# Eleven tiny SyncE loads and sixteen small GpSimd loads added in mid-kernel to a rotary-embedding score kernel

## The chip, the cores and the metric

The kernel runs on one core of one Trainium2 chip. The time is device microseconds of one launch. What lies in a profile is one execution; the timed runs are others of the same program.

## The reference

Queries and keys of 16 batches, 512 positions, 16 heads and 64 elements are rotated by position-dependent cosines and sines, and for every batch and position the 16 heads' queries are multiplied with the keys of the same head:

```python
q_rot = concat([q1 * cos - q2 * sin, q1 * sin + q2 * cos])   # q1, q2: halves of the 64 elements
k_rot = concat([k1 * cos - k2 * sin, k1 * sin + k2 * cos])
scores = einsum('bshd,bthd->bsht', q_rot, k_rot)             # fp32, 16 x 512 x 16 x 512
```

The output has 268 MB, the two inputs 67 MB together; both go through the core's DMA engines once.

## The kernel before

The 512 positions of a batch are dealt over 128 partitions, four to a partition: `C = 4`. A step handles one such quarter of a batch, 128 query positions against all 512 key positions for all 16 heads, so there are `NST = 64` steps, four a batch. The first four (batch 0) have a form of their own with smaller loads and stores; the others, from step 4 to step 63, are one loop.

In a step `i` of the loop, `scores(i, p, st)` runs for eight pairs of heads `p`: two matrix products into a PSUM tile (line 166), and a ScalarE copy of both into the staging tile `st` (line 173). Between the pairs, TensorE transposes the rotated queries of step `i + 1` and a quarter of the keys of the batch after (line 127), and VectorE or ScalarE copies them out of PSUM (line 142). VectorE's rotations (lines 106, 107 and 111) for the steps ahead are woven in between, the rest of them in `run(dve)` at the end of the step.

After the last pair of a step, `store(i, st)` writes the staging tile, 4 MB, to `out`. A staging tile is 32 KB a partition, and there are three of them (`stage_pool`, `bufs=3`), so ScalarE's first copy of step `i` waits until the store of step `i - 3` has landed. Two steps, `NST - 8 = 56` and `NST - 1 = 63`, write in three pieces: all 128 rows of most heads, then 116 rows and 12 rows of the last two (step 56) or three (step 63) heads:

```python
nc.sync.dma_start(o[:, :h], st[:, :h])
nc.sync.dma_start(o[:116, h:], st[:116, h:])
nc.sync.dma_start(o[116:, h:], st[116:, h:])
```

At the end of step `i`, after `run(dve)`, the loop issues a load: with `i % 4 == 2` the queries of batch `i // 4 + 2`, with `i % 4 == 3` the keys of batch `i // 4 + 3`, each 2 MB, into one of two buffers. Step 50 thus issues the queries of batch 14, step 54 those of batch 15. All loads and stores but two at the start (`cos`, `sin`) are issued by SyncE, in program order: store 50, the queries of batch 14, store 51, a load of keys, stores 52, 53 and 54, the queries of batch 15, store 55, the three pieces of step 56, and so on. Nothing is issued by GpSimd, which only builds the identity matrix at the start.

The order of the instructions on each engine is that of the program text (`tc.manual_schedule()`); the waits between engines and DMAs are put in by the framework from what each instruction reads and writes.

Of the kernel before, what the change touches and what calls it, by code (L numbers as in the profile page):

```python
# [10 lines left out]
def kernel(  # L11
# [8 lines left out]
    nc = tc.nc  # L20
    fp32 = mybir.dt.float32
# [5 lines left out]
    P = 128  # L27
    C = S // P
    HP = H // 2
    NST = B * C  # L30
    G = H // C

    const_pool = ctx.enter_context(tc.tile_pool(name="const", bufs=1))
# [16 lines left out]
    cos_t = const_pool.tile([P, C, HD], fp32, name="cos_t")  # L50
# [2 lines left out]
    ss_v = ss_t.rearrange("p c x j -> p c (x j)")  # L53

    st_first = [stage_pool.tile([P, H, S], fp32, tag="stage", name="st") for _ in range(2)]
    early = stage_pool.tile([P, 2 * C * H * D], fp32, tag="stage", name="early")
# [3 lines left out]
    def load_units(which, head, heads):  # L62
        n = C * heads * D
        t = early[:, used[0] : used[0] + n].rearrange("p (c e) -> p c e", c=C)
        used[0] += n
        src = dram[which][0, :, :, head : head + heads, :]
        nc.sync.dma_start(t.rearrange("p c (h d) -> p c h d", d=D), src)
        for h in range(0, heads, G):
            units[which, (head + h) // G] = t[:, :, D * h : D * (h + G)]
# [3 lines left out]
    def load(which, b):  # L73

        if b >= B:
            return
        t = in_pool.tile([P, C, H * D], fp32, tag=which + "_in", name=which + "_sb")
        batches[which, b] = t
        nc.sync.dma_start(t.rearrange("p c (h d) -> p c h d", h=H), dram[which][b])

    def rope(which, n):

        part = part_pool.tile([P, H * D], fp32, tag="part", name="part")
        if n < C:
            x = units[which, n]
            sv, k1, k2 = "p c (g j) -> p c g j", {"j": HD}, {"j": D}
            cs = cos_t.unsqueeze(2).to_broadcast((P, C, 2 * G, HD))
            ss = ss_v.unsqueeze(2).to_broadcast((P, C, G, D))
            pv = part.rearrange("p (c g j) -> p c g j", c=C, j=D)  # L90
            x5 = x.rearrange("p c (h x j) -> p c h x j", x=2, j=HD)
            p5 = part.rearrange("p (c h x j) -> p c h x j", c=C, x=2, j=HD)
            adds = [(x5[:, :, :, y], p5[:, :, :, 1 - y]) for y in range(2)]
        else:
            x = batches[which, n // C][:, n % C]
            sv, k1, k2 = "p (g j) -> p g j", {"j": HD}, {"j": D}
            cs = cos_t[:, n % C].unsqueeze(1).to_broadcast((P, 2 * H, HD))
            ss = ss_v[:, n % C].unsqueeze(1).to_broadcast((P, H, D))
            pv = part.rearrange(sv, **k2)
            x4 = x.rearrange("p (h x j) -> p h x j", x=2, j=HD)  # L100
            swapped = bass.AP(part.tensor, part.offset + HD, [part.ap[0], (D, H), (-HD, 2), (1, HD)])
            adds = [(x4, swapped)]
        xs, xc = x.rearrange(sv, **k2), x.rearrange(sv, **k1)

        def products():
            nc.vector.tensor_tensor(pv, xs, ss, op=mult)  # L106
            nc.vector.tensor_tensor(xc, xc, cs, op=mult)  # L107

        def sums():
            for y, z in adds:  # L110
                nc.vector.tensor_tensor(y, y, z, op=add)  # L111

        return [products, sums]
# [41 lines left out]
    def scores(i, p, st):  # L155

        ps = ps_s_pool.tile([P, 2, S], fp32, tag="ps_s", name="ps")
        b = i // C
        if b == 0:
            c, hp = divmod(p, 2)  # L160
            lhs, rhs = qT[i][:, C * hp + c], kT[0][:, 2 * i + hp]
        else:
            lhs, rhs = qT[i][:, p], kT[b][:, p]
        for r in range(2):
            po, rh = ps[:, r, :], rhs[64 * r : 64 * r + 64, :]
            nc.tensor.matmul(  # L166
                out=po, lhsT=lhs[64 * r : 64 * r + 64, :], rhs=rh, start=True, stop=True
            )
        so, si = st[:, 2 * p : 2 * p + 2, :], ps
        if b > 0:  # L170
            so = so.rearrange("s r (t c) -> s r t c", c=C)
            si = si.rearrange("s r (c t) -> s r t c", c=C)
        nc.scalar.copy(out=so, in_=si)  # L173
        if b == 0 and p % 2 == 1:
            c = p // 2
            nc.sync.dma_start(o_v[0, c, :, G * i : G * (i + 1)], st[:, G * c : G * (c + 1)])
        elif b > 0 and p == HP - 1:
            store(i, st)

    def tr_act(which, n):  # L180
        for g in range(2):
            transposed(which, n, g, nc.scalar.copy)

    def run(ops):
        for op in ops:
            op()

    with tc.manual_schedule():
        for t, src in ((cos_t, cos), (sin_t, sin)):
            nc.scalar.dma_start(t, src.rearrange("(p c) j -> p c j", c=C))  # L190
        for head, heads in ((0, G), (G, H - G)):
            load_units("k", head, heads)
            load_units("q", head, heads)
        load("k", 1)
        load("q", 1)
        make_identity(nc, ident)
        nc.scalar.copy(out=ss_t[:, :, 0, :], in_=sin_t)
        nc.scalar.mul(ss_t[:, :, 1, :], sin_t, -1.0)  # L198
        for which in ("k", "q"):
            run(rope(which, 0))  # L200
            tr_act(which, 0)

        for i in range(C):
            st = st_first[i] if i < 2 else stage_pool.tile([P, H, S], fp32, tag="stage", name="st")
            if i < C - 1:
                dve = rope("k", i + 1) + rope("q", i + 1) + rope("k", C + i)
                nxt = [("k", i + 1), ("q", i + 1)]
            else:
                dve = rope("q", C) + rope("k", C + i) + rope("q", C + 1) + rope("k", 2 * C)  # L210
                nxt = [("q", C), ("k", C + i)]
            for p in range(HP):
                scores(i, p, st)
                if p in (0, 1) and i > 0:
                    run(dve[:1])
                    dve = dve[1:]
                    transposed("k", C + i - 1, p, nc.vector.tensor_copy)
                if p == 3 and i < 2:
                    load("kq"[i], 2)
                if p in (2, 6):  # L220
                    m = len(dve) - (4 if p == 2 else 2) - (2 if i == C - 1 else 0)
                    run(dve[:m])
                    dve = dve[m:]
                    tr_act(*nxt.pop(0))
            run(dve)
        load("k", 3)

        for i in range(C, NST):
            tr = {}  # L230
            if i + 1 < NST:
                tr[1], tr[3] = ("q", i + 1, 0), ("q", i + 1, 1)
            if i + C < NST:
                tr[5], tr[6] = ("k", i + C, 0), ("k", i + C, 1)
            dve = []
            if i + 2 < NST:
                dve += rope("q", i + 2)
            if i + 1 + C < NST:
                dve += rope("k", i + 1 + C)
            st = stage_pool.tile([P, H, S], fp32, tag="stage", name="st")  # L240
            for p in range(HP):
                scores(i, p, st)
                if p not in tr:
                    continue
                if tr[p][0] == "q":
                    run(dve[:1])
                    dve = dve[1:]
                    transposed(*tr[p], nc.vector.tensor_copy)
                else:
                    transposed(*tr[p], nc.scalar.copy)  # L250
            run(dve)
            if i % C == C - 2:
                load("q", i // C + 2)
            elif i % C == C - 1:
                load("k", i // C + 3)
# [30 lines left out]
```

## Time and profile before

| | us |
|---|---|
| median of 2 runs (799.76 and 801.14) | 800.45 |
| profiled execution, span from its first to its last instruction | 798.6 |
| TensorE busy | 690.1 (86%) |
| ScalarE busy | 561.3 (70%) |
| VectorE busy | 544.5 (68%) |
| GpSimd busy | 0.7 |
| mean DMA rate | 421 GB/s |
| a 4 MB store, issue to landing, median | 24.1 |
| a 2 MB load, issue to landing, median | 27.6 |

The profiled execution has no time of its own beside its span; the two runs lie 1.2 and 2.5 us above the span, for what comes before the first and after the last instruction. Busy times of different engines overlap. TensorE's busy time counts pipelined matrix products whose ends are modelled. A DMA's time from issue to landing includes its time in the queue behind the DMAs issued before it.

### The profile page before, as it was taken

The page shows a single profiled execution, that of the slowest core. Times are in us where ns is not written, and L with a number is a line of the kernel's source. Part 1 is how long each engine was busy: PE and PEld are TensorE (multiplying, and loading weights), DVE is VectorE, ACT ScalarE, POOL GpSimd, SP SyncE. Part 2 cuts the span into 40 slices and gives each one's busy share as a digit, 9 for nine tenths or more (in the row PEclk, how much of TensorE's full clock was granted, in tenths as well). Part 3 has the DMA queues.
Part 4 walks back from the last instruction along what each step waited for, and adds up shares of the span by engine and source line. Part 5 has one row for each costly group of instructions (what it writes and reads, how often), then busy time and mean ns, then how long its engine had stood idle before and what let it go on. Part 6 is the DMA issues. An engine that isn't in the chain of part 4 may idle for free.

```text
span 798.6 us, 7719 instructions
## 1 busy us (share of the span) xinstructions
PE 690.1 (86%) x3072; PEld 299.2 (37%) x3072; DVE 544.5 (68%) x516; ACT 561.3 (70%) x647; POOL 0.7 (0%) x6
## 2 busy tenths in 40 slices
PE   4999998997979789797897988979889798899970
PEld 2444443433434334343343433424334243344420
DVE  7999987676857568575685766857758577586300
ACT  3888886776848668485785866858668586688770
POOL 0000000000000000000000000000000000000000
PEclk9999999899989899898998998999989899899995
DMA  9999999999999999999999999999999999999995
GB/s 357 421 411 435 437 423 433 423 427 440 421 431 429 429 437 427 436 421 434 426 432 434 431 420 429 434 429 437 427 424 407 443 422 440 423 404 419 426 426 235
DMA packets 17988, 336.17 MB, mean 421 GB/s; under 512 B 1824, under 2 KB 3104, under 8 KB 4384
## 3 DMA queue, kind: packets, MB, share of 16 engines
q1 hardware_dynamic: 17664, 335.55, 98.7%
q8 instruction: 24, 0.39, 0.2%
q10 hardware_dynamic: 288, 0.13, 0.1%
q14 instruction: 12, 0.10, 0.0%
HBM read 67.24 MB, written 268.44 MB: 420 GB/s over the span
## 4 chain that ended last, share of the span: by engine, by line
DMA 51%; PE 38%; ACT 4%; DVE 3%; issue 1%; ACTq 0%; SPq 0%
DMA out_dram<-st 48%; PE ps L166 29%; PE bank L127 9%; ACT st L173 4%; DMA q_sb<-in_q_dram 2%; DVE part L106 1%; DMA sin_t<-in_sin_dram 0%; DVE q_sb L107 0%; DVE k_sb L111 0%; DVE k_sb L107 0%; DVE q_sb L111 0%; DVE early L107 0%; DVE kT_t L142 0%; ACTq L281 0%; DVE early L111 0%
## 5 line engine op out<-in xcount | busy, mean ns | idle before, releaser
L173 ACT COPY st<-ps 128x1024 f32<-128x1024 f32 x512 | 495.0, 1019 | 203.4 <-DMA out_dram<-st 112.3
L166 PE MATMUL ps<-kT_t,qT_t 64*128 64x512 f32 x2048 | 547.9, 653 | 72.1 <-ACT st L173 72.1
L166 PEld LDWEIGHTS ps<-kT_t,qT_t 64*128 64x128 f32 x2048 | 185.0, 197 | 261.9 <-issue 140.6
L142 DVE COPY qT_t<-bank 128x512 f32<-128x512 f32 x118 | 81.5, 691 | 203.8 <-PE bank L127 203.8
L127 PEld LDWEIGHTS bank<-ident,q_sb 128*128 128x128 f32 x480 | 55.5, 151 | 102.4 <-issue 99.8
L127 PE MATMUL bank<-ident,q_sb 128*128 128x128 f32 x480 | 86.7, 308 | 0.9 <-PE ps L166 0.9
L127 PEld LDWEIGHTS bank<-ident,k_sb 128*128 128x128 f32 x480 | 50.5, 141 | 95.0 <-DVE k_sb L107 37.5
L127 PE MATMUL bank<-ident,k_sb 128*128 128x128 f32 x480 | 78.7, 287 | 1.2 <-DVE qT_t L142 1.2
L142 ACT COPY kT_t<-bank 128x512 f32<-128x512 f32 x122 | 72.5, 599 | 6.2 <-PE bank L127 6.2
L107 DVE TENSOR_TENSOR q_sb<-q_sb,cos_t 128x1024 f32<-128x1024 f32 x60 | 73.5, 1225 | 2.1
L111 DVE TENSOR_TENSOR k_sb<-k_sb,part 128x1024 f32<-128x1024 f32 x60 | 73.5, 1225 | 2.1
L107 DVE TENSOR_TENSOR k_sb<-k_sb,cos_t 128x1024 f32<-128x1024 f32 x60 | 73.5, 1225 | 2.0
L106 DVE TENSOR_TENSOR part<-q_sb,ss_t 128x1024 f32<-128x1024 f32 x60 | 73.5, 1225 | 2.0
L106 DVE TENSOR_TENSOR part<-k_sb,ss_t 128x1024 f32<-128x1024 f32 x60 | 73.0, 1216 | 0.1
L111 DVE TENSOR_TENSOR q_sb<-q_sb,part 128x1024 f32<-128x1024 f32 x60 | 72.9, 1216 | 0.0
L127 PE MATMUL bank<-ident,early 128*128 128x128 f32 x64 | 10.5, 316 | 12.3 <-DVE early L111 10.4
L127 PEld LDWEIGHTS bank<-ident,early 128*128 128x128 f32 x64 | 8.3, 161 | 17.3 <-issue 13.2
L106 DVE TENSOR_TENSOR part<-early,ss_t 128x1024 f32<-128x1024 f32 x8 | 9.8, 1223 | 5.7 <-ACT ss_t L198 5.5
L111 DVE TENSOR_TENSOR early<-early,part 128x512 f32<-128x512 f32 x16 | 10.3, 687 | 0.2
L107 DVE TENSOR_TENSOR early<-early,cos_t 128x1024 f32<-128x1024 f32 x8 | 9.8, 1225 | 0.3
L142 ACT COPY qT_t<-bank 128x512 f32<-128x512 f32 x10 | 5.7, 630 | 3.2 <-PE bank L127 3.2
L142 DVE COPY kT_t<-bank 128x512 f32<-128x512 f32 x6 | 4.1, 684 | 0.0
(9 smaller groups left out, 2.8 us busy)
## 6 DMA issues: line engine op xcount, KB each, us to landing
out_dram<-st SPq DMA_DIRECT2D x58, 4096.0 KB, 24.1
k_sb<-in_k_dram SPq DMA_DIRECT2D x15, 2048.0 KB, 27.6
q_sb<-in_q_dram SPq DMA_DIRECT2D x15, 2048.0 KB, 27.6
out_dram<-st SPq DMA_DIRECT2D x16, 1024.0 KB, 13.7
out_dram<-st SPq DMA_DIRECT2D x1, 3584.0 KB, 22.8
out_dram<-st SPq DMA_DIRECT2D x1, 3328.0 KB
early<-in_k_dram SPq DMA_DIRECT2D x1, 1536.0 KB, 8.8
early<-in_q_dram SPq DMA_DIRECT2D x1, 1536.0 KB, 12.0
```

What stands on the lines that cost most here:

```text
L106: nc.vector.tensor_tensor(pv, xs, ss, op=mult)
L107: nc.vector.tensor_tensor(xc, xc, cs, op=mult)
L111: nc.vector.tensor_tensor(y, y, z, op=add)
L127: nc.tensor.transpose(bank[:, x, :], src, ident)
L142: copy(out=dst, in_=src)
L166: nc.tensor.matmul(out=po, lhsT=lhs[64 * r : 64 * r + 64, :], rhs=rh, start=True, stop=True)
L173: nc.scalar.copy(out=so, in_=si)
```

## The change

Two small helpers are added, and called in three places. `probe(counts)` issues tiny loads on SyncE, each of 8 columns (32 bytes) of a few rows of `cos` into a tile of its own; the count 1 stands for 17 rows. `burden()` makes one small ScalarE copy into a tile `sw`, and then sixteen times [...]issues a GpSimd load of 17 rows, two pieces of 104 elements (416 bytes) each, into the same part of `sw`. Nothing reads `hw` or `sw` afterwards. Step 50 gets the loads of 5 to 11 rows and the sixteen GpSimd loads, between `run(dve)` and the load of the queries of batch 14; step 54 gets the loads of 17, 2, 3 and 4 rows, ahead of the load of the queries of batch 15. All else stays.

```diff
+    hw = [const_pool.tile([P, 8], fp32, name=f"hw{n}") for n in range(12)]
+    sw = const_pool.tile([P, 224], fp32, name="sw")
+    PROBE = NST - 14
+
+    def probe(counts):
+        for n in counts:
+            rows = 17 if n == 1 else n
+            nc.sync.dma_start(hw[n][:rows, :], cos[:rows, :8])
+
+    def burden():
+        nc.scalar.copy(out=sw[:, :8], in_=cos_t[:, 0, :8])
+        for n in range(16):
+            nc.gpsimd.inc_swdge_sem([], [], mode="reset_dge_cursor")
+            src = bass.AP(q.tensor, 2048 * n, [(4096, 17), (512, 2), (1, 104)])
+            nc.gpsimd.dma_start(sw.rearrange("p (a b) -> p a b", a=2)[:17, :, :104], src)
...
             run(dve)
+            if i == PROBE:
+                probe((5, 6, 7, 8, 9, 10, 11))
+                burden()
+            if i == PROBE + 4:
+                probe((1, 2, 3, 4))
             if i % C == C - 2:
                 load("q", i // C + 2)
```

## The prediction

> **What bounds the kernel now.** I read the page first, then SyncE's own waits, its timeline around step 50, the store's line, and the stages.
>
> ```profile
> span 798.6 us, 7719 instructions
> ...
> DMA  9999999999999999999999999999999999999995
> ...
> q1 hardware_dynamic: 17664, 335.55, 98.7%
> ...
> DMA 51%; PE 38%; ACT 4%; DVE 3%; issue 1%; ACTq 0%; SPq 0%
> ...
> L173 ACT COPY st<-ps 128x1024 f32<-128x1024 f32 x512 | 495.0, 1019 | 203.4 <-DMA out_dram<-st 112.3
> ```
>
> The reader is to see a kernel held by the 16 DMA engines: they are busy in every slice, nearly all of it with SyncE's queue (q1), and ScalarE's largest idle time ends when a store lands and frees a staging buffer. So whatever makes a DMA engine idle or gives it more work is paid, unless that engine has slack.
>
> The page hides that the 16 engines are not level. The trace's landing events show each engine's share of a store: store 49 lands between 635.00 and 645.53 us, store 50 between 644.75 and 655.54. Ten to eleven shares come within about a microsecond of the first; one engine trails by 10.8 us. Leading engines keep their lead only while the queue holds work. The laggard is not the one that ends the kernel: it has its last full share at 790.32, while the four engines that carry the 116-row pieces of steps 56 and 63 run to 797.28. They are busy without a gap from 708 us on.
>
> ```profile
> SPq L147 <- ACT st L173: 645.8, 58, 16.3
> ```
>
> ```profile
> L147 SPq EVENT_SEMAPHORE  x58: 17/17/17, 62.9 to 757.4; - x58
> L147 SPq DMA_DIRECT2D out_dram<-st x58: 332/332/360, 73.2 to 766.9; - x58
> ...
> DMA to landing us min/median/max: 16.5/24.1/30.3
> ```
>
> The first line is the longest of SyncE's own waits (total, times, longest): the stores wait for ScalarE, and no wait for a DMA is listed but the final one. The others are the store's line. Each of the 58 whole stores has one event-semaphore instruction ahead of it. In the trace's operands it waits for the semaphore that the store itself will raise when it lands. SyncE's DMAs take eight such semaphores in turn (I call them lanes 0 to 7), so a DMA is issued only once the DMA eight places earlier has landed. With eight DMAs reaching back some 50 us against a largest landing time of 30.3, this costs nothing today, and no such wait is in the list.
>
> ```profile
> 630.07 0.33 SPq L147 DMA_DIRECT2D out_dram<-st  x1
> 630.50 0.66 SPq L79 DMA_DIRECT2D q_sb<-in_q_dram  x1
> 647.02 0.33 SPq L147 DMA_DIRECT2D out_dram<-st  x1
> 647.45 0.45 SPq L79 DMA_DIRECT2D k_sb<-in_k_dram  x1
> 657.04 24.43 SPq L147 DMA_DIRECT2D out_dram<-st  x3
> 681.57 0.82 SPq L79 DMA_DIRECT2D q_sb<-in_q_dram  x1
> ```
>
> Those are store 50, the q load of batch 14, store 51, a k load, stores 52 to 54, the q load of batch 15. The seven step-50 loads of the change go between the first two lines.
>
> ```profile
> 635.76 2.84 ACT L173 COPY st<-ps 128x1024 f32<-128x1024 f32 x3 [5.72 <-DMA out_dram<-st]
> ```
>
> ```profile
> 646.00:658.00 12.00, 12.00 (x60) 5.23 (x56) 9.40 (x9) 10.67 (x13) 0.00 (x0) 1.00 1.01 436
> 658.00:700.00 42.00, 36.87 (x155) 15.49 (x153) 27.02 (x26) 27.41 (x32) 0.00 (x0) 0.88 1.00 430
> ```
>
> First ScalarE's timeline at the end of step 50, then two stages; DMA share and GB/s stand last. There is no DMA hole at 646 to 658 today.
>
> [...] one 4-byte completion packet per engine used makes 112 x 16 for all full DMAs, ACT's two among them, plus 4 + 12 + 4 + 12 for the split ones, 1824, the page's count under 512 B. The 12-row piece's shares land 0.18 us after the 116-row piece's on the same four engines. No run here shows a GpSimd DMA. [...]
>
> **Part 1: the SyncE loads and their lanes.** Store 50 holds lane 7. The 5 to 11-row loads take lanes 0 to 6, whose earlier holders are store 45, store 46, a q load, store 47, a k load, store 48 and store 49. The first five have landed by 625.7. The sixth load waits for store 48 (635.66), the seventh for store 49 (645.53). Behind them stands the q load, which now falls on lane 7 itself and waits for store 50, the DMA issued just before: 655.54 instead of 630.50. Store 51, its data ready at 647.02, stands behind that. So the ring holds nothing after store 50 but rows of 32 B.
>
> The leading engines finish store 50 at 644.75 and start again at 657.5 (issue at 655.6, then the 2.0 us that store 47 took from its issue at 598.38 to its first share's start, 610.10 less eight packets of 1.213). That is 12.7 us of idle. The laggard idles 2 us. Afterwards all are level. Can the four final engines win it back? In the kernel before they had about 0.45 us of further starvation (at 698 to 708), so no. Their ends lay between 795.6 and 797.3 because of their own lag of up to 1.7 us, which the pause levels: all arrive at about 797.3 + 12.7 - 0.45 - 1.7 = 807.9. That is +10.6. I checked the rest of the chain for a second hole: store 51 now lands at about 673 (before 670.4), store 54 is issued near 683, the next ones at some 699, 707 and 719, each 8 us or more before the ring runs dry.
>
> The issues themselves, 7 x 0.33 to 0.66 us and 4 more at step 54, lie in SyncE's own idle time (631 to 647, and after 682, with work queued until about 696). At step 54 the lanes asked for hold store 51 and the k load, landed by about 680: nothing. The descriptors are 27 on the first engine, at 9 ns (4-byte packets) to 27 ns (512-byte ones): 0.2 to 0.7, I take 0.3 us. If the pause weren't there, these issues would still cost nothing.
>
> **Part 2: ScalarE's copy** of 128x8 is below the 0.6 us of a 128x512 one, and falls into its 5.72 us of waiting at 630 to 636: nothing.
>
> **Part 3: the GpSimd loads.** 16 loads of 17 rows x 2 pieces of 416 B are 544 packets. Packet times are 27 ns at 512 B, 46 at 1 KB, 309 at 8 KB, 1213 at 32 KB, or some 8 ns + 37 ns per KB: 23 to 24 ns each, 0.83 us a load, 13.2 us in all. [...] all of them weigh on one engine, which I take to be the first: one of the four that end the kernel. All write the same tile, so I expect each to wait for the one before. One load then takes: descriptor making and landing, bounded by the 1.6 us from issue to first landing of the small cos load[...], 0.8 us of packets, and one to four turns behind a 1.2 us store packet. That is 3 us in the pause and 4.5 to 8 us otherwise. From 631 to 657.5 I count 4.5 loads; those are hidden by the pause. The other 11.5 x 0.83 = 9.5 us are added to an engine that never idles again. The chain ends near 735, well before the kernel. Bounds: 0 (all inside the pause, or another engine) to 13.2; above if packets are dearer.
>
> **Sum.** 10.6 + 0.3 + 9.5 = 20.4 us on a span of 798.6, or 819.0. The median of the runs, 800.45, lies 1.85 above the span; the same surplus gives 820.9, so 821.
>
> **Rivals.** *A, mostly the pause (chance 0.32).* The GpSimd loads are dealt two rows to an engine (nine engines, 64 packets each: 1.5 us), or are not serialized and run in the pause. [...] Time 800.45 + 10.9 + 1.5 = 812.9. This is the case on the other side, within 2%: it decides once fewer than six loads (5.1 us / 0.83) run after 657.5.
>
> *B, the chain outlives the kernel (0.15).* If an engine alternates single pieces with 32 KB store packets, a load takes 34 x 1.24 = 42 us plus 3. By 808 about seven are done; the other nine take 3.5 us each in an empty queue, 32 us: 842. For: store packets are single rows. [...]
>
> *C, SyncE isn't held (0.06),* because small shapes raise their lanes otherwise. Then only GpSimd's 13.2 us or 1.5 remain: 801 to 814. Against: the wait instruction is on every store.
>
> **Chances.** Main case 0.45, and 0.02 for something that helps. Of the main case 0.05 stays below 816.5 (some 2%, about what a measurement here can tell from no change). Slower: 0.40 + 0.15 + 0.03 of unnamed mishaps = 0.58; same: 0.05 + 0.32 + 0.03 = 0.40; faster 0.02. The range reaches from 808, below A with a cheap restart, to 842, B's value.
>
> **What would show it.** SyncE's waits list DMA waits of about 13 and 10 us at the small loads and the q load; the q load's issue at about 655.6; DMA share far below 1 between 646 and 658; packets below 512 B up by 544 + 16 x 16 and the small rows; the last store's landing near 817; later in the kernel ScalarE waiting for stores that one engine holds back. Wrong, if the q load is still issued near 634, if the GpSimd packets end before 660, or if they run on after the last store.

## The result, and the profile after

The changed kernel took 821.81 us (821.03 and 822.59) against 800.45 before: 1.027 of it, with an interval of 1.0236 to 1.0304, or 21.4 us more. The prediction said 821. The total is met more closely than its terms: the pause was put some 3 us too low and the GpSimd loads some 3 us too high, as the experiments show.

The page of the changed kernel, the lines that answer to those of before and two more:

```profile
span 819.3 us, 7767 instructions
...
DMA  9999999999999999999999999999999499999993
GB/s 358 420 424 430 433 419 439 420 432 429 431 435 429 425 430 434 431 425 438 421 434 428 429 436 427 436 423 432 434 424 434 204 392 435 394 422 375 424 406 133
...
q1 hardware_dynamic: 17812, 335.55, 96.6%
q0 software_dynamic: 1280, 0.26, 0.2%
```

The DMA row was full from end to end; now its 32nd slice of forty (635 to 655 us) is at 4, with 204 GB/s. After it the rate stays below that of before although the busy digit is 9 again. Those are two places to look for the loss: a hole, and slower going after it. The new queue q0, GpSimd's, has 1280 packets, which is 16 loads x 16 engines x 5. By their sizes in the trace a load has three packets of 4160 B and one of 1664 B, which are ten, ten, ten and four pieces of 416 B; 45 packets of 40 B and 15 of 16 B, which fits three and one for each of the fifteen other engines; and 16 completion packets of 4 B. SyncE's queue q1 has 148 packets more than before, 82 rows of 32 B and 66 completion packets of 4 B, both of 9 ns (median). By the landing events each tiny load has a share for every row, but that of 17 rows a single one (landed 710.54): 56 + 9 + 1 = 66.

SyncE's own waits in the changed kernel (total, times, longest), and its timeline:

```profile
SPq L64 <- DMA out_dram<-st: 10.0, 2, 9.4
SPq L95 <- DMA out_dram<-st: 9.9, 1, 9.9
```

```profile
628.49 0.33 SPq L163 DMA_DIRECT2D out_dram<-st  x1
628.88 15.53 SPq L64 DMA_DIRECT2D hw<-in_cos_dram  x7
654.37 0.36 SPq L95 DMA_DIRECT2D q_sb<-in_q_dram  x1
654.83 0.38 SPq L163 DMA_DIRECT2D out_dram<-st  x1
655.31 0.37 SPq L95 DMA_DIRECT2D k_sb<-in_k_dram  x1
655.77 29.89 SPq L163 DMA_DIRECT2D out_dram<-st  x3
```

Line 64 is the tiny load, line 95 the load of queries or keys, line 163 the store. The seven tiny loads stretch over 15.5 us, because the last two wait: the sixth for store 48 (landed 634.10, load issued 634.12), the seventh for store 49 (landed 644.10, issued 644.12). The load of queries behind them is issued at 654.37, 0.07 us after store 50's last share landed (654.30 by the landing events); in the kernel before it stood 0.43 us behind the store's own issue. By the operands in the trace the seven tiny loads wait for the semaphores 100, 101, 102, 103, 105, 107 and 109, each for the one that it raises itself, and ahead of the load of queries stands a wait for 110, which is store 50's. Store 51 and the keys follow at once: they had been ready, and were held only by SyncE's order.

The stages of the changed kernel (busy time of each engine, then granted clock, DMA share, GB/s):

```profile
632.00:646.00 14.00, 10.73 (x44) 4.69 (x44) 6.73 (x6) 9.85 (x12) 0.96 (x1) 0.88 0.85 359
646.00:658.00 12.00, 12.00 (x58) 5.18 (x57) 10.37 (x10) 10.15 (x12) 1.93 (x2) 1.00 0.30 93
658.00:700.00 42.00, 31.35 (x132) 13.49 (x132) 23.04 (x22) 23.56 (x28) 3.64 (x4) 0.84 1.01 423
700.00:730.00 30.00, 24.80 (x114) 10.38 (x111) 19.70 (x19) 20.64 (x25) 2.14 (x3) 0.91 1.00 408
```

In 646 to 658 TensorE is busy for all of the 12 us and ScalarE for 10, while the DMA share is 0.30, against 1.01 in the same stage of the kernel before: nothing that computes was late, only the DMA queue was empty. There is a second, smaller hole: from 751 to 754 the DMA share is 0.35 at 144 GB/s, after ScalarE had waited 6.44 and 3.77 us for stores (until 726.65 and 741.19) and a store was issued only at 753.24. The slowest engines had work all the while: the store before lands on the first engine at 751.0 and on the last at 761.0. GpSimd's timeline, in part (in brackets the idle time before a load and what ended it):

```profile
640.75 0.96 POOL L71 DMA_DIRECT2D sw<-in_q_dram  x1 [10.82 <-DMA sw<-in_q_dram]
651.99 0.96 POOL L71 DMA_DIRECT2D sw<-in_q_dram  x1 [10.27 <-DMA sw<-in_q_dram]
656.08 0.96 POOL L71 DMA_DIRECT2D sw<-in_q_dram  x1 [3.12 <-DMA sw<-in_q_dram]
666.10 0.96 POOL L71 DMA_DIRECT2D sw<-in_q_dram  x1 [9.06 <-DMA sw<-in_q_dram]
...
798.29 0.96 POOL L71 DMA_DIRECT2D sw<-in_q_dram  x1 [11.80 <-DMA sw<-in_q_dram]
```

Each load waits for the one before. The third, issued at 651.99 while most engines are idle, lands 3.8 us later; behind stores a load takes about 11 us (median of the sixteen 11.5). In the sixth load, behind stores, the four large packets start at 681.38, 682.74, 684.11 and 685.48, each as long after the one before as one of them and one 32 KB store packet take (0.16 + 1.21 us); in the third they start at 653.69, 653.85, 654.13 and 654.29, one after another. Thirteen come after the hole, and the last lands at 809.8, before the last store piece at 818.3.

### The profile page after: what moved, and what is told of

Read it like the earlier page. It is cut to its first block, busy times and chain, and to the rows that moved or that the text cites. A ratio compares the mean times of both kernels' runs of the same rounds, so it can differ in the third digit from the quotient of the medians.

```text
span 819.3 us, 7767 instructions
## 1 busy us (share of the span) xinstructions
PE 690.4 (84%) x3072; PEld 300.2 (37%) x3072; DVE 544.6 (66%) x516; ACT 561.7 (69%) x648; POOL 16.2 (2%) x22
## 3 DMA queue, kind: packets, MB, share of 16 engines
q0 software_dynamic: 1280, 0.26, 0.2%
## 4 chain that ended last, share of the span: by engine, by line
issue 95%; POOL 2%; POOLq 0%
POOL sw L71 2%; POOLq L302 0%; POOLq L69 0%; POOL ident masks.py:199 0%; POOL ident masks.py:197 0%; POOLq masks.py:199 0%; POOLq L291 0%
## 5 line engine op out<-in xcount | busy, mean ns | idle before, releaser
L122 DVE TENSOR_TENSOR part<-k_sb,ss_t 128x1024 f32<-128x1024 f32 x60 | 73.0, 1216 | 0.1
L127 DVE TENSOR_TENSOR q_sb<-q_sb,part 128x1024 f32<-128x1024 f32 x60 | 72.9, 1216 | 0.0
L71 POOL DMA_DIRECT2D sw<-in_q_dram x16 | 15.5, 970 | 782.4 <-ACT sw L67 627.6
```

Of the source, the lines that this page charges most:

```text
L71: nc.gpsimd.dma_start(sw.rearrange("p (a b) -> p a b", a=2)[:17, :, :104], src)
```

## The experiments

Theory: eight landing semaphores taken in turn (lanes; in the trace of the changed kernel 100 to 103, 105, 107, 109 and 110, with 15 or 16 DMAs each) make SyncE wait, the wait empties the DMA engines, and the GpSimd loads then weigh on one engine that ends the kernel. Rivals: the pause is won back, the pause is all, the loads cost by their mere count. Ratios are to runs of the kernel before on the same chip.

**The SyncE loads alone.** The line `burden()` is left out.

> The eleven tiny SyncE loads at steps 50 and 54 alone, without the ScalarE copy and the GpSimd loads. Theory (lane pause): the queries' load still waits for store 50, the 16 engines run dry between about 643 and 657 us, and the kernel takes 800.45 + 10.9 = about 811 us; in the profile the load is issued in the same tenth of a microsecond in which store 50 lands. Rival (the GpSimd loads make nearly all of the 21 us, the pause is won back by later slack): within 3 us of 800. Rival (the pause makes nearly all): 818 or more.

Measured 815.0 us, 1.0170 (1.0153 to 1.0187): 14.1 more than the 800.9 beside it. The load of queries is issued at 656.17, store 50's last share had landed at 656.09, and two stages of it read

```profile
646.00:660.00 14.00, 14.00 (x68) 5.92 (x64) 11.67 (x12) 12.15 (x14) 0.00 (x0) 1.00 0.29 97
660.00:700.00 40.00, 29.62 (x125) 12.61 (x125) 21.62 (x22) 22.18 (x27) 0.00 (x0) 0.83 1.01 424
```

The profiled execution is the longest of the four (818.25 us, with a span of 816.5). The pause is there without any GpSimd load, and it isn't won back. It costs 3 us more than expected, about its whole length: the first share of store 50 lands at 644.95, the first share of the load of queries at 663.90. Its eight packets take 0.611 us each in a full queue, so 14.0 us lie between 644.95 and the 659.0 at which they would have had to start.

**The GpSimd loads alone.** Both calls of `probe` are left out.

> The ScalarE copy and the 16 GpSimd loads at step 50 alone, no tiny SyncE loads. Theory (one engine that ends the kernel takes all the data): no pause, so all 16 loads are paid, at 0.55 us of packets each (in the profile of the changed kernel: three of 161 ns and one of 69 ns)[...]: 16 x 0.85 = 13.6, about 814 us. If the engine were one with slack of 7 to 9 us at the end: 805 to 808. Rival (the pause is all): 800 to 802. If both parts simply add, this and the run with the SyncE loads alone give together the 21.4 us of the whole change; with three loads hidden in the pause their sum should be 2 to 3 us more.

Measured 812.99, 1.0147 (1.0120 to 1.0174). The number is near the expected one, the reason only half so. Of the 0.85 us a load behind it 0.55 is measured (three packets of 161 ns and one of 69); the other 0.3, here and at step 30, was the author's estimate, shown by no trace. And in the profiled execution, the longest of the four at 815.19, the last store piece landed at 808.2, and the chain of loads ended at 811.9, after it. GpSimd's last two loads:

```profile
801.47 0.96 POOL L71 DMA_DIRECT2D sw<-in_q_dram  x1 [9.92 <-DMA sw<-in_q_dram]
809.17 0.97 POOL L71 DMA_DIRECT2D sw<-in_q_dram  x1 [6.74 <-DMA sw<-in_q_dram]
```

So 3.7 us of that execution are a chain that outlives the stores, as in rival B of the prediction; in the changed kernel the stores end later and hide it. How much of the median's 12.1 us it makes wasn't measured. The two parts alone make 14.1 + 12.1 = 26.2 us, 4.8 more than the whole change, where 2 to 3 more were expected.

**Five tiny loads.** At step 50 `probe((5, 6, 7, 8, 9))`, nothing else of the change.

> Only five of the tiny loads at step 50 (5 to 9 rows), nothing at step 54 and no GpSimd loads. Lane theory: the queries' load then stands on the lane of store 48 (landed at about 635), store 51 on that of store 49 (landed at 645, before its data are ready at 647), the keys' load on that of store 50, which still leaves it 2 us before the queue runs dry. So no pause: 800 to 801 us, although five of the seven loads are there. Rival (tiny loads themselves disturb the engines, each by about 1.5 us): 808.

**Six tiny loads.** At step 50 `probe((5, 6, 7, 8, 9, 10))`, nothing else.

> As the run with five, with the load of 10 rows added: six. Lane theory: the queries' load waits for store 49 (about 645.5), 2.8 us of empty queue on the leading engines, and store 51 waits for store 50 (about 655.5), 5.1 us more after the queries have been loaded: 7.9 us of pause less 2 us of lag that it levels, about 806 us. Rival (each tiny load costs the same): a seventh of the way more than with five, about 809 to 810, in line with it. Rival (only the wait of the queries' load counts): 802.

Five: 801.10, 1.0004 (0.9996 to 1.0013), no difference. Six: 808.34, 1.0091 (1.0076 to 1.0107), 2 us more than expected. SyncE's timeline of the two around step 50, five first:

```profile
631.30 0.33 SPq L163 DMA_DIRECT2D out_dram<-st  x1
631.69 4.83 SPq L64 DMA_DIRECT2D hw<-in_cos_dram  x5
636.63 1.15 SPq L95 DMA_DIRECT2D q_sb<-in_q_dram  x1
645.36 0.37 SPq L163 DMA_DIRECT2D out_dram<-st  x1
654.63 0.33 SPq L95 DMA_DIRECT2D k_sb<-in_k_dram  x1
```

```profile
629.55 0.33 SPq L163 DMA_DIRECT2D out_dram<-st  x1
629.93 5.88 SPq L64 DMA_DIRECT2D hw<-in_cos_dram  x6
645.48 0.36 SPq L95 DMA_DIRECT2D q_sb<-in_q_dram  x1
655.53 0.37 SPq L163 DMA_DIRECT2D out_dram<-st  x1
656.00 0.37 SPq L95 DMA_DIRECT2D k_sb<-in_k_dram  x1
```

With five, the keys' load waits for store 50 (landed 654.6), and still comes in time; with six, the load of queries waits for store 49 and store 51 for store 50. The stage 646 to 658, five and then six:

```profile
646.00:658.00 12.00, 12.00 (x60) 5.46 (x60) 9.91 (x10) 10.15 (x13) 0.00 (x0) 1.00 1.03 437
```

```profile
646.00:658.00 12.00, 12.00 (x60) 5.30 (x58) 9.40 (x10) 10.67 (x13) 0.00 (x0) 1.00 0.70 274
```

Nothing, 7.4 and 14.1 us for five, six and seven at step 50: a threshold and then a step for each load, where a cost by the load would have shown at five. Each load more moved every DMA behind it one place closer to the one that it had to wait for: the load of queries is issued at 636.63 with five, at 645.48 behind store 49 with six, and at 656.17 behind store 50 with seven.

**The same eleven, dealt.** `probe((5, 6, 7, 8, 9))` at step 50, `probe((1, 2, 3, 4))` at step 54, `probe((10, 11))` at step 58, no `burden()`.

> All eleven tiny SyncE loads, but those of 10 and 11 rows moved from step 50 to the end of step 58; no ScalarE copy and no GpSimd loads. Lane theory: with five at step 50, four at step 54 and two at step 58 every lane that is asked for has landed, or just lands, so no pause: 800 to 802 us, against 815 for the same eleven loads with seven of them at step 50. Rival (the loads' descriptors and issues cost it): about 815 again.

Measured 800.87, 1.0007 (1.0000 to 1.0015). All eleven loads together cost 0.6 us by the ratio and 1.2 at most by its interval, where no more than five stand in a row. The lane theory passes its sharpest test here: the same loads cost 14.1 us when seven stand in a row.

**Step 56 stored whole** (an edit of the kernel before).

```diff
-        if i not in (NST - 8, NST - 1):
+        if i != NST - 1:
```

> The kernel before with one edit: step 56 is stored whole, as the other steps are, instead of in three pieces; no tiny and no GpSimd loads. It tells which engines end the kernel before. As the prediction read the landings (only the four engines with the 116-row pieces end it, the laggard is done at 790.32): those four lose 5.9 + 0.2 us of pieces and get 1.2 us of whole rows, so about 796. As I read them now, with the extra semaphore events put aside (the laggard[...] has its last full share at 797.0, as late as the four): the laggard gets 8 x (1.213 - 1.062) us more and saves its one 12-row packet of 0.2, so 801 to 802, or 0.1% slower.

Measured 800.16, 1.0000 (0.9992 to 1.0009). The first reading, 796, falls. The second's direction can't be told at this size, but the landings agree with it: the laggard's last full share lands at 797.1, the four engines end between 795.7 and 796.8.

**Pieces of one element.** In `burden()`, `(1, 104)` becomes `(1, 1)` and `[:17, :, :104]` becomes `[:17, :, :1]`.

> The changed kernel with each GpSimd piece cut from 104 elements (416 B) to one (4 B); 16 loads of 34 pieces as before, so the load's count, its waits and its turns stay, its bytes go. The changed kernel took 21.4 us more than before, the SyncE loads alone 14.1 in the run with them alone: the GpSimd loads' own part is about 7. Theory (the bytes on one engine): the 13 loads after the pause lose 13 x 0.5 us of packets, so about 815. Rival (turns: a load breaks into the stores' queue on every engine, whatever its size): unchanged, 821. In between, some 817 to 818, if both count.

**No cursor reset.** The line `nc.gpsimd.inc_swdge_sem(...)` is left out.

> The changed kernel without the 16 resets of the GpSimd cursor; the loads are the same. Theory (with the reset all data go to one engine, without it they go round): each engine gets the data of one load, 0.55 us, instead of one engine that of 16; about 816. Rival (the cursor has no part in where the data go, or the engine has no part in the cost): unchanged, 821.

Without bytes: 820.21, 1.0246 (1.0231 to 1.0261). Without resets: 821.18, 1.0270 (1.0245 to 1.0295). Both intervals overlap that of the changed kernel. So neither the bytes nor their lying on one engine make most of the GpSimd part; the theory in this form falls. The run without bytes also has fewer packets, two a load on every engine (136 B and 4 B) instead of five, and its chain of loads ends at 770.3 instead of 809.8; still it costs 5.2 us more than the SyncE loads alone. So the number of packets doesn't make most of it either. What stays is 34 pieces a load on every engine, if one reads the sizes so, which is the author's reading: 136 B is 34 x 4, and 40 and 16 B on the other engines are 10 x 4 and 4 x 4. No run here varied the number of pieces. The stages of the run without bytes, at the same distance from the pause as those of the SyncE loads alone, show what is left:

```profile
660.00:700.00 40.00, 28.86 (x116) 12.33 (x116) 21.20 (x20) 20.57 (x24) 4.82 (x5) 0.79 1.01 419
700.00:740.00 40.00, 36.67 (x170) 15.79 (x166) 28.25 (x27) 29.35 (x35) 3.86 (x4) 0.96 1.00 404
```

against this second stage of the SyncE loads alone:

```profile
700.00:740.00 40.00, 35.83 (x164) 15.33 (x160) 29.67 (x28) 27.76 (x34) 0.00 (x0) 0.96 1.00 426
```

The engines are busy all the time in both, and move 426 or 404 GB/s. Between 700 and 780 us the stores' 32 KB packets take 1219 ns in the mean in the run with the SyncE loads alone and 1251 in the one without bytes, the loads' 16 KB packets 621 and 726.

**A place of its own for each load.** In `burden()`, `[:17, ...]` becomes `[r : r + 17, ...]` with `r = 17 * (n % 7)`.

> The changed kernel with the GpSimd loads written to seven groups of 17 partitions in turn instead of all to the first 17, so that up to seven are in flight and none waits for the one just before it. [...] Theory (what is done while the engines are held empty at 643 to 657 us costs nothing): the loads are issued about 1 us apart and nearly all done by 660, and the time is that of the SyncE loads alone, 815 to 816. Rival (a GpSimd load costs the stores the same wherever it runs): unchanged, 821. In the profile the last GpSimd load should start near 650 to 665 instead of 798.

Measured 819.05, 1.0231 (1.0216 to 1.0246): between the two, so neither expectation came. GpSimd's timeline tells why:

```profile
631.64 6.83 POOL L72 DMA_DIRECT2D sw<-in_q_dram  x7 [630.33 <-ACT sw L67]
643.68 0.96 POOL L72 DMA_DIRECT2D sw<-in_q_dram  x1 [5.21 <-DMA sw<-in_q_dram]
647.86 0.96 POOL L72 DMA_DIRECT2D sw<-in_q_dram  x1 [3.22 <-DMA sw<-in_q_dram]
654.21 0.96 POOL L72 DMA_DIRECT2D sw<-in_q_dram  x1 [5.38 <-DMA sw<-in_q_dram]
655.89 5.77 POOL L72 DMA_DIRECT2D sw<-in_q_dram  x6 [0.72 <-DMA sw<-in_q_dram]
```

A load lands only with the last of its 16 shares (those of the second in the changed kernel from 643.6 to 651.7), and the slowest engine was here still at store 50 until 655. So the last six were issued only as the pause ended, met the stores again, and landed between 667 and 693. Six loads at the 0.6 us that the next run gives would make 3.6 of the 4.0 us by which this run exceeds the SyncE loads alone.

**Four GpSimd loads.** `range(16)` becomes `range(4)`.

> The changed kernel with 4 GpSimd loads instead of 16. In the changed kernel the first three landed by 656 us and the fourth was issued at 656. Theory (loads that run while the engines are held empty are free, the others cost 0.3 to 0.6 us each): the SyncE loads' own 814 to 815, at most 1 us more. Rival (the GpSimd loads lengthen the pause itself, or their first use costs something once): 818 or more, most of the 7 us that sixteen add.

Measured 814.44, 1.0175 (1.0160 to 1.0191), the same as without any. The first loads are free, in the pause and before it; the other twelve cost 821.8 - 814.4 = 7.4 us, 0.6 each. The two runs of the changed kernel leave almost 3 us either way; with the 821.18 of the run without resets it is 6.7.

**The GpSimd loads at step 30**, without SyncE loads: `if i == PROBE - 20: burden()`, and the same **without resets**.

> No SyncE loads; the ScalarE copy and the 16 GpSimd loads moved from step 50 to step 30, where their chain (about 11 us a load) ends near 570 us, long before the stores end, and no pause lies near. Theory (bytes on one of the engines that end the kernel): that engine loses 16 x (0.55 + 0.3) = 13.6 us and has at most a few of slack, so 809 to 814. Rival (turns: each load takes about 0.33 us from every engine, as the store-by-store rates of the earlier runs say, and the bytes hide behind the lag of the slowest engine): 16 x 0.33 = 5.3, so about 806. Rival (the cost is only the chain's end and what it meets in the tail): 801.

> As the run with the GpSimd loads at step 30, without the 16 cursor resets[...]. Theory (bytes on one engine): the bytes are dealt, 0.55 us an engine, and only turns remain: 5 to 6 us, about 806, clearly below the run with the resets. Rival (turns alone): the same as the run with the resets.

With resets 807.46, 1.0093 (1.0076 to 1.0111); without 803.79, 1.0050 (1.0031 to 1.0070). Here the intervals part: of 7.0 us, 3.4 stay without resets, and 3.6 come with them. The last landings show what these are: with resets one of the four engines with 116-row pieces ends at 804.3 and the others by 801.7, without resets all four between 800.3 and 801.3. That fits bytes on one engine with resets and bytes dealt without them. Neither time is quite the expected one (809 to 814 or 806, and 806). Three stages of the run with resets, in which the chain is at work, and the same stages of the kernel before:

```profile
380.00:440.00 60.00, 53.05 (x230) 22.46 (x226) 41.47 (x39) 40.01 (x47) 4.93 (x5) 0.91 1.00 421
440.00:500.00 60.00, 51.88 (x222) 22.14 (x224) 39.13 (x37) 42.17 (x49) 4.82 (x5) 0.89 1.00 418
500.00:560.00 60.00, 53.75 (x250) 23.27 (x248) 43.86 (x42) 45.07 (x53) 4.83 (x5) 0.97 1.00 418
```

```profile
380.00:440.00 60.00, 52.70 (x229) 22.34 (x230) 40.23 (x38) 41.35 (x49) 0.00 (x0) 0.91 1.00 430
440.00:500.00 60.00, 54.34 (x229) 23.16 (x229) 40.91 (x38) 42.15 (x49) 0.00 (x0) 0.89 1.00 426
500.00:560.00 60.00, 54.17 (x250) 23.71 (x250) 43.44 (x42) 44.73 (x52) 0.00 (x0) 0.94 1.01 431
```

At the same full DMA share the rate is 9, 8 and 13 GB/s lower, 30 of 1287, or 4.2 us in these 180; five loads are issued in each stage, so about 0.28 us a load in the mean of the engines. Without resets the same stages move 423, 421 and 419 GB/s. The laggard's last full share moves from 797.0 to 801.1, as it should if every engine pays. The packets of 380 to 560 us show where the time goes: GpSimd's own fill 24 us of the 16 engines' time, about a third of the loss (16 x 4.2 us). The rest is in SyncE's packets, which take longer beside them: 660 instead of 626 ns in the mean for 16 KB, 1228 instead of 1217 for 32 KB. Why they do is open.

## Why the prediction was right, and where not

*The DMA engines bound the kernel, and an empty queue is paid.* Right. TensorE's and ScalarE's busy times are those of before (690.4 and 561.7 us) and the whole loss is in DMA stages.

*The lanes.* Right, in place and order: waits of 10.0 us in all at the tiny loads (9.4 of them at the seventh) and 9.9 at the load of queries, where 13 and 10 were told, issue within 0.1 us of store 50's landing, DMA share 0.30. The run with five, the run with six and the dealt run show that the waits, not the loads, are the cost. Rival C is out. Nothing came from step 54, as told.

*The size of the pause.* Too small: +10.6 told, +14.1 measured alone. Two terms failed. The restart was put at 2.0 us, as for a store in the kernel before; by the same reckoning the load of queries took 2.8 (issue at 654.37, and 662.08 - 4.89 = 657.2), so the leading engines lost 14.3 us, from 642.9, and not 12.7. This reckoning isn't the true start: in the trace the load's first packets start at 655.36, 1.0 us after the issue, but the first on each engine takes 0.85 to 1.7 us where one of this size takes 0.61 in a full queue. And 2.15 us were credited for lag and starvation that the pause would level. The pause does level the engines: the shares of the load land within 1.0 us of each other. But they drift apart again. In the run with the SyncE loads alone the four 116-row pieces of step 56 end between 735.2 and 739.4, and those of step 63 at 809.3, 809.9, 810.9 and 815.3. Its profile is of an execution 3 us over the median; in the run with four GpSimd loads, profiled close to its median, they end between 808.8 and 811.4. So the credit came for the first of the four engines at most, and the last one ends the kernel.

*"The laggard is not the one that ends the kernel."* Wrong, a misreading of the trace. In the trace of the kernel before, each 116- and 12-row piece has an extra semaphore event (the 116-row piece of step 56 five for its four shares: one at 707.84 and those of the shares from 722.27 to 723.90), which shifted the later landings by one or two. With these put aside the laggard's last full share lands at 797.0, as late as the four engines. The run with step 56 stored whole was made for this, and didn't gain the 4 us of the first reading. The sum was little hurt, because after the pause the laggard is level with the rest and no longer decides.

*The GpSimd loads.* Told 9.5 us; sixteen cost 6.8 beside the SyncE loads alone, and 7.4 beside four. That a load's bytes lie on one engine was an assumption there, and the trace bears it out: ten pieces in a packet can't be two rows to an engine, which have four, so rival A's dealing is out; the large packets start one store packet apart behind stores (the sixth load) and one after another beside idle engines (the third); and the late engine of the run at step 30 is one of the four that end the kernel. Three terms were mis-sized. Packets: the pieces went ten to a packet, not singly, three packets of 161 ns and one of 69 a load by the trace, 0.55 us instead of 0.83. Speed: the 3 us in the pause and 4.5 to 8 otherwise were the author's estimate; the load that ran beside idle engines took 3.8 us, one behind stores about 11, so three were hidden and not 4.5, and the chain ended at 809.8, not near 735. And a term was put at nothing: a load also has 60 packets of 40 and 16 B beside its four large ones, and SyncE's packets beside the loads took longer (660 instead of 626 ns for 16 KB at step 30), together 0.28 us of lost rate in the mean of the engines. GpSimd's queue has 1216 packets under 512 B where 544 + 256 were told. The mechanism of one burdened engine is real at step 30 (3.6 us of 7.0), but after the pause the runs can't separate it from noise. Why the bytes on one engine count for so little there, when 13 loads of 0.55 us should make 7, is open; the uneven 116-row pieces, which end last, may cover it, but no run shows it.

*The sum.* 10.6 + 0.3 + 9.5 was 20.4; the runs give 14.1 for the SyncE loads and about 7 for the others. The 3.5 us missing in one and the 2.5 too many in the other nearly cancel, and that 821 was met so closely is luck. Rival A had the measured order of the parts, with the pause the larger, but would have left GpSimd's share at 1.5.

## What to carry to other kernels

Count landing semaphores as a resource: SyncE's DMAs took eight in turn here, so each small load moved every later DMA closer to the one that it had to wait for, and seven of them behind a 4 MB store stopped an otherwise full queue (DMA share 0.30 from 646 to 658 us; 14.1 us in the run with the SyncE loads alone). Dealt out, at most five in a row, the same loads were all but free (0.6 us). And read a DMA share together with its GB/s: between 700 and 740 us a share of 1.00 at 404 instead of 426 GB/s was a loss that the busy digit hid.

## What the runs showed that was not expected

A GpSimd load of 17 rows has its bytes on one engine but packets on all sixteen (1280 packets for 16 loads). It lands only with its last share, and the shares of the second load land from 643.6 to 651.7. Behind a queue of stores it took about 11 us, for 14 KB.

The pieces of 116 rows take very different times on their four engines (in the changed kernel the shares of step 56's land at 735.99, 738.20, 739.04 and 740.89): in the trace a 4 KB packet has a median of 159 ns, a mean of about 200 and, in the changed kernel, a largest of 799. In the run with the SyncE loads alone one of the four ended 4.4 us after the next; that the uneven packets are the cause isn't shown.
